# Latents' gates four blocks at a time in the banks of rows' sums, those banks then holding the input of the u products, and context's v rows on VectorE

## The chip, the cores and the metric

The kernel runs on one core of a Trainium2 chip. The metric is the device time of one execution in microseconds (us); of several runs the median is taken.

## The reference, cut to what matters

A two-layer backbone in float32 over 256 context tokens and 256 latent tokens, width 1024. In the kernel these are four tiles of 128 tokens: tiles 0 and 1 are context, 2 and 3 latents. In each layer four branches (two attentions, a convolution, a pooling) are merged under gates, and then a layer of experts follows, in which each token takes 128 rows of 1024 numbers out of a table u and 128 out of a table v (8 heads, 16 rows each, out of 16384 rows):

```python
def merge_branches(h, ys, w_gate, b_gate, w_branch, w_out):
    acc = jax.nn.sigmoid(h @ w_gate[0] + b_gate[0]) * (ys[0] @ w_branch[0])
    for n in range(1, N_BRANCH):
        acc = acc + jax.nn.sigmoid(h @ w_gate[n] + b_gate[n]) * (ys[n] @ w_branch[n])
    return acc @ w_out

def peer_ffn(h, wq, k1, k2, u_tab, v_tab):      # for 128 tokens xc
    ...
    u = jnp.take(u_tab, idx, axis=0)
    act = jax.nn.gelu(jnp.einsum('td,thkd->thk', xc, u), approximate=False)
    v = jnp.take(v_tab, idx, axis=0)
    return jnp.einsum('thk,thkd->td', gate * act, v)
```

Context goes through the experts in the first layer only, so there are six gathers of 128 slots (one slot: one u row and one v row for each of 128 tokens): here called C0, L0, L1, C1 (first layer: context tile 0, latent tiles 2 and 3, context tile 1) and F0, F1 (second layer, latents).

## The kernel before, in words

**Order.** The program is written out in one function, and the order of its lines is the order in which work is offered to the engines. It starts with context's first layer (`both` on `hc`). Then latents' first layer runs, with gather C0 laid between its products: `pump(us)` counts up the products' time and at every SLOT_US (2.9) steps the generator `gather` one slot on; `tick` does the same for pieces of attention, convolution and pooling in `pending`. Gathers L0 and L1 run alone, beside the router's selection of rows. C1 is laid between the products of latents' second layer, F0 begins beside the last products of that layer, and F1 runs alone to the end.

**A gather's slot.** `u_slot` (L1128) has GpSimd issue an indirect DMA (L1124) of one u row per token into a place of tag "u", and VectorE multiply it with the tile's normed input `self.h2` and sum it up (L1132). `v_slot` (L1142) fetches the v rows 16 slots later. A v row is either added up on VectorE into `dacc` (L1149), or ScalarE makes a diagonal matrix of its weights (L1154) and TensorE adds two products of 512 columns up in PSUM (L1156). `on_dve` says which: P_C0 sends 122 of C0's rows to VectorE, `few` a quarter, `half` a half, `most` (C1) three quarters; the last row is always TensorE's. At the end `add` (L1166) weighs the sums and adds them to X, once for `dacc` and once for PSUM. `prepare` (L1102) makes `h2` out of X, in SBUF, with a product and a sum (L1110, L1113).

**PSUM.** All eight banks have a tag: mm (2 tiles of one bank), at (2), tr (2) and va (one tile of two banks, the v rows' sums, held through a whole gather).

**Gates.** In latents' first layer `both` (L954) loads, for each half c of the columns and branch n, one weight tile of w_branch and two of w_gate (1024 x 256 each), all 1 MB in the three places of tag "w". It goes block by block: `gate_mm` (8 products of 256 columns, then a tanh on ScalarE), then `branch_mm` (4 products, then VectorE's product with the gate, L941, and sum, L942). In the second layer `both_quads` (L967) does four blocks at a time: `gate_quad` loads two tiles of w_gate (512 x 512 each) and runs half of the depth of all four blocks out of the first and the other half out of the second, into two mm tiles, followed by four tanh; then w_branch is loaded, and two times two blocks of branch products go into a tr tile (L975), each followed by one product and one sum on VectorE with 512 columns (L984, L985). The gates of four blocks stand in two tiles of tag t2, of which there are four, and from which attention takes its own tiles too.

## Time and profile before

| | us |
|---|---|
| median of 3 runs | 3176.56 |
| lowest, highest | 3165.32, 3186.99 |
| the profiled execution | 3168.74 |
| its span | 3167.0 |

The profile is of one execution. Busy time over the span: TensorE 75%, VectorE 74%, GpSimd 56%, ScalarE 21%; the kernel moves 1036 MB, 327 GB/s on the mean. These are averages over stages with different limits, so the profile is read by stage. The stages stand in it at: latents' first layer with C0 about 415 to 1020 us, L0 to 1410, L1 to 1800, latents' second layer with C1 to 2280, the end of that layer to 2380, F0 to 2790, F1 to the end. "POOL" in a row is GpSimd, "PE" TensorE, "DVE" VectorE, "ACT" ScalarE, "SP" the queue that loads weights.

### The profile page before, as it was taken

The numbers are of one execution on the slowest core, as the hardware profiler recorded it, in microseconds if no ns is written. First come the engines' busy times: TensorE is split into PE (matmuls) and PEld (weight loads), VectorE is DVE, ScalarE is ACT, GpSimd is POOL, SyncE is SP. The second block draws the span as 40 slices with busy tenths as digits, with TensorE's granted clock in tenths as the row PEclk, the third lists the DMA queues.
The fourth block names the chain that finished last, engine by engine and source line by source line (L and its number), as shares of the span: only waits on it lengthen the run. The fifth ranks groups of instructions, "written<-read, shape, count | busy, mean of one in ns | idle before, by whom it ended". The sixth has DMA issues, their size and how long they took to land.

```text
span 3167.0 us, 32196 instructions
## 1 busy us (share of the span) xinstructions
PE 2376.9 (75%) x10264; PEld 1586.2 (50%) x10264; DVE 2357.8 (74%) x5204; ACT 654.6 (21%) x1543; POOL 1789.3 (56%) x1542
## 2 busy tenths in 40 slices
PE   7999989898877785665455589899997966645555
PEld 5879878666666452222111267667696522211111
DVE  5977679678968899747666769977567985566666
ACT  3454321233112211110000211123332211100001
POOL 0000057443556687776777757766205777777775
PEclk9999999899988897886777789899998988876767
DMA  9948979787999899998999999999838989999998
GB/s 305 334 161 285 304 263 351 270 296 250 339 331 356 321 392 364 336 381 294 373 369 369 338 343 389 341 388 386 300 107 288 323 324 372 372 344 372 383 377 300
DMA packets 397863, 1036.48 MB, mean 327 GB/s; under 512 B 30464, under 2 KB 169216, under 8 KB 397696
## 3 DMA queue, kind: packets, MB, share of 16 engines
q0 software_dynamic: 221184, 805.40, 68.0%
q1 hardware_dynamic: 173072, 226.25, 21.0%
q10 hardware_dynamic: 3440, 2.78, 0.3%
q8 instruction: 82, 1.34, 0.2%
q14 instruction: 85, 0.70, 0.1%
HBM read 1032.22 MB, written 2.10 MB: 327 GB/s over the span
## 4 chain that ended last, share of the span: by engine, by line
PE 33%; DVE 18%; issue 17%; DMA 15%; POOL 15%; ACT 1%; another core or an unknown queue 0%; POOLq 0%; SPq 0%; ACTq 0%; DVEq 0%
PE mm L218 11%; POOL u L1124 8%; POOL v L1124 7%; DMA v<-in_v_dram,idx 7%; DVE u L1132 5%; PE va L1156 4%; DMA w<-in_w_gate_dram 3%; PE mm L214 3%; PE mm L216 2%; PE mm L215 2%; PE mm L916 2%; DMA u<-in_u_dram,idx 2%; DVE dacc L1149 2%; PE at L531 2%; DVE m L832 2%
## 5 line engine op out<-in xcount | busy, mean ns | idle before, releaser
L1124 POOL DMA_INDIRECT u<-in_u_dram,idx x768 | 869.7, 1132 | 926.4 <-DVE m L862 409.0
L1156 PE MATMUL va<-v,dg 128*128 128x512 f32 x1436 | 890.5, 763 | 554.5 <-DMA v<-in_v_dram,idx 379.8
L1132 DVE SCALAR_TENSOR_TENSOR u<-u,h 128x1024 f32<-128x1024 f32 x768 | 933.2, 1219 | 338.1 <-DMA u<-in_u_dram,idx 307.6
L1124 POOL DMA_INDIRECT v<-in_v_dram,idx x768 | 919.1, 1197 | 433.6 <-issue 193.9
L1156 PEld LDWEIGHTS va<-v,dg 128*128 128x128 f32 x1436 | 315.8, 237 | 1070.4 <-issue 925.6
L1149 DVE SCALAR_TENSOR_TENSOR dacc<-v,wt,dacc 128x1024 f32<-128x1024 f32 x403 | 515.6, 1279 | 105.9 <-DMA v<-in_v_dram,idx 78.6
L218 PE MATMUL mm<-hT,w 128*128 128x256 f32 (+1 forms) x1664 | 383.4, 385 | 71.4 <-DMA w<-in_w_gate_dram 50.9
L218 PEld LDWEIGHTS mm<-hT,w 128*128 128x128 f32 x1664 | 312.4, 207 | 130.2 <-issue 53.6
L1154 ACT ACTIVATE dg<-ident,wt 128x128 f32<-128x128 f32 x359 | 141.3, 400 | 1029.9 <-PE va L1156 524.7
L832 DVE SCALAR_TENSOR_TENSOR m<-m,cols,m 128x256 f32<-128x256 f32 x360 | 158.2, 473 | 0.1
L916 PE MATMUL mm<-hT,w 128*128 128x256 f32 x512 | 134.5, 405 | 14.5 <-DVE t L453 6.6
L215 PE MATMUL mm<-hT,whi 128*128 128x256 f32 x512 | 143.4, 280 | 0.0
L214 PE MATMUL mm<-hT,whi 128*128 128x256 f32 x448 | 128.0, 286 | 3.1 <-ACT whi L176 3.1
L216 PE MATMUL mm<-hT,whi 128*128 128x256 f32 x448 | 127.2, 284 | 1.8 <-DVE whi L177 1.8
L218 PE MATMUL mm<-w,hT 128*128 128x256 f32 x512 | 117.1, 388 | 10.6 <-DMA w<-in_w_in_dram 10.6
L916 PEld LDWEIGHTS mm<-hT,w 128*128 128x128 f32 x512 | 97.6, 202 | 34.5 <-issue 17.2
L177 DVE TENSOR_TENSOR whi<-w,whi 128x1024 fp32r<-128x1024 f32 x86 | 103.6, 1220 | 13.8 <-ACT whi L176 6.5
L218 PEld LDWEIGHTS mm<-w,hT 128*128 128x128 f32 x512 | 99.1, 195 | 26.4 <-issue 12.5
L176 ACT CAST whi<-w 128x1024 fp32r<-128x1024 f32 x86 | 87.4, 1047 | 51.3 <-PE mm L216 20.6
L215 PEld LDWEIGHTS mm<-hT,whi 128*128 128x128 f32 x512 | 97.0, 190 | 0.4 <-issue 0.3
L214 PEld LDWEIGHTS mm<-hT,whi 128*128 128x128 f32 x448 | 85.3, 190 | 8.8 <-ACT whi L176 4.2
L216 PEld LDWEIGHTS mm<-hT,whi 128*128 128x128 f32 x448 | 84.8, 189 | 7.2 <-DVE whi L177 3.7
(361 smaller groups left out, 2960.9 us busy)
## 6 DMA issues: line engine op xcount, KB each, us to landing
w<-in_w_gate_dram SPq DMA_DIRECT2D x48, 1024.0 KB
w<-in_w_in_dram SPq DMA_DIRECT2D x42, 1024.0 KB
X<-in_w_mod_dram SPq DMA_DIRECT2D x40, 512.0 KB
wm<-in_w_mod_dram SPq DMA_DIRECT2D x40, 512.0 KB
w<-in_w_branch_dram SPq DMA_DIRECT2D x20, 1024.0 KB
w<-in_w_q_dram SPq DMA_DIRECT2D x20, 1024.0 KB
u<-in_u_dram,idx POOLq DMA_INDIRECT x768
v<-in_v_dram,idx POOLq DMA_INDIRECT x768
```

The source lines that it names most:

```text
L177: nc.vector.tensor_tensor(lo.bitcast(FR), v, hi, op=OP.subtract)
L214: nc.tensor.matmul(ps, ah, bh, start=first, stop=False)
L215: nc.tensor.matmul(ps, ah, bl, start=False, stop=False)
L216: nc.tensor.matmul(ps, al, bh, start=False, stop=last)
L218: nc.tensor.matmul(ps, a[:, kb, ca], b[:, kb, cb], start=first, stop=last)
L832: nc.vector.scalar_tensor_tensor(acc[:, b, :], yb[:, b, k:k + T], cols[:, l, cw + k:cw + k + 1], acc[:, b, :], op0=OP.mult, op1=OP.add)
L916: nc.tensor.matmul(ps, a[:, kb, ca], b[:, k0 + kb, cb], start=f, stop=z, skip_group_check=True)
L1124: nc.gpsimd.indirect_dma_start(out=r, out_offset=None, in_=table, in_offset=bass.IndirectOffsetOnAxis(ap=self.idx[:, j:j + 1], axis=0))
L1132: nc.vector.scalar_tensor_tensor(r, r, 1.0, self.h2, op0=OP.mult, op1=OP.mult, accum_out=self.act[:, j % 16:j % 16 + 1])
L1149: nc.vector.scalar_tensor_tensor(self.dacc, v, w, self.dacc, op0=OP.mult, op1=OP.add)
L1154: nc.scalar.activation(dg, ident, AF.Copy, scale=w)
L1156: nc.tensor.matmul(self.va[:, half, :], dg, v[:, half * 512:(half + 1) * 512], start=j == self.pe[0], stop=j == self.pe[-1])
```

## The change

Four things, the third of which follows from the second:

- Latents' first layer calls `both_quads` in place of `both`, with the ticks and pumps per block as they were.
- `gate_quad` puts its four blocks into the two banks of va, and `both_quads` its branch products into mm tiles in place of tr tiles (both layers).
- These banks are then free for the gathers of latents: the last sum of `prepare` writes `h2` of a latent tile into va, where L1132 reads it for 128 rows; the sums of v rows on TensorE go into two at tiles. For context `h2` stays in SBUF.
- Context's gathers C0 and C1 have no row on TensorE: all 128 v rows are summed up on VectorE, and there is one `add` in place of two. That takes 6 rows of C0 and 33 of C1 (every fourth and the last) off TensorE.

```diff
@@ -919,7 +919,9 @@ gate_quad
-        ps = [mm_ps() for i in range(2)]
+
+        ps = va_ps()
+        ps = [ps[:, :512], ps[:, 512:]]
@@ -972,7 +974,7 @@ both_quads
-                    pb = tr_ps()
+                    pb = mm_ps()
@@ -1101,22 +1103,25 @@ Tile
         def prepare(self, found=False):
 
-            self.h2 = sb.tile([128, D], F, tag="h2", name="h2", bufs=2)
+            h2 = sb.tile([128, D], F, tag="h2", name="h2", bufs=2)
+
+            self.h2 = va_ps() if self.t > 1 else h2
...
-                nc.vector.scalar_tensor_tensor(self.h2[:, c], X[:, self.t, c], rst2[:, self.t:self.t + 1], ps,
+                nc.vector.scalar_tensor_tensor(h2[:, c], X[:, self.t, c], rst2[:, self.t:self.t + 1], ps,
                                                op0=OP.mult, op1=OP.mult)
                 ps = bcast(tr_ps(), modc[self.l][:, self.s, 24 + half * 4:28 + half * 4])
-                nc.vector.tensor_tensor(self.h2[:, c], self.h2[:, c], ps, op=OP.add)
+                nc.vector.tensor_tensor(self.h2[:, c], h2[:, c], ps, op=OP.add)
 
         def begin(self, on_dve):
 
-            self.pe = [j for j in range(128) if not on_dve(j) or j >= 128 - LAST]
+
+            self.pe = [j for j in range(128) if not on_dve(j) or j >= 128 - LAST] if self.t > 1 else []
             self.dv = [j for j in range(128) if j not in self.pe]
-            self.va = va_ps().rearrange("p (a b) -> p a b", a=2)
+            self.va = [at_ps() for half in range(2)] if self.pe else None
...
                 if j == self.dv[-1]:
-                    self.add(self.dacc)
+                    self.add([self.dacc[:, :512], self.dacc[:, 512:]])
...
-                    nc.tensor.matmul(self.va[:, half, :], dg, v[:, half * 512:(half + 1) * 512],
+                    nc.tensor.matmul(self.va[half], dg, v[:, half * 512:(half + 1) * 512],
...
-        t.add(t.va.rearrange("p a b -> p (a b)"))
+        if t.pe:
+            t.add(t.va)
...
-    P_C0, P_L0, P_L1, P_C1, P_F0, P_F1 = (lambda j: j < 48 or (j * 15) % 16 < 15), few, half, most, few, half
+    P_L0, P_L1, P_F0, P_F1 = few, half, few, half
...
-    behind.append(gather(tsc[0], P_C0, None, rc))
+    behind.append(gather(tsc[0], None, None, rc))
@@ -1426,17 +1432,17 @@ latents, first layer
-    both(h, ys, T, 0, (3,), accT, True)
+    both_quads(h, ys, 0, (3,), accT, True)
...
-    both(h, ys, T, 0, (0,), accT, False)
+    both_quads(h, ys, 0, (0,), accT, False)
...
-    both(h, ys, T, 0, (1,), accT, False)
+    both_quads(h, ys, 0, (1,), accT, False)
...
-    both(h, ys, T, 0, (2,), accT, False)
+    both_quads(h, ys, 0, (2,), accT, False)
...
-    behind.append(gather(tsc[1], P_C1))
+    behind.append(gather(tsc[1], None))
```

## Rows read from the trace of the kernel before

**Rows 1.** Busy time by stage (columns: stretch, length, each engine's busy us, clock, DMA share, GB/s)

```profile
620.00:925.00 305.00, 259.34 (x1188) 206.76 (x1188) 250.85 (x579) 76.11 (x180) 143.54 (x122) 0.92 0.82 293
1020.00:1300.00 280.00, 196.21 (x567) 108.70 (x566) 268.10 (x892) 50.19 (x118) 208.81 (x170) 0.84 0.95 356
1300.00:1410.00 110.00, 75.12 (x147) 29.61 (x146) 58.91 (x87) 14.27 (x38) 86.52 (x78) 0.86 0.97 358
1410.00:1800.00 390.00, 208.24 (x314) 73.84 (x312) 256.57 (x377) 35.67 (x93) 287.26 (x262) 0.71 0.94 353
1990.00:2280.00 290.00, 265.85 (x1183) 196.45 (x1182) 214.80 (x366) 81.23 (x205) 181.01 (x147) 0.94 0.95 357
2600.00:2790.00 190.00, 128.95 (x243) 50.66 (x244) 96.82 (x142) 24.87 (x62) 139.00 (x133) 0.84 0.97 367
...
1500.00:1550.00 50.00, 25.67 (x36) 8.58 (x36) 35.33 (x51) 3.03 (x8) 38.11 (x40) 0.78 1.03 407
```

**Rows 2.** TensorE's waits, 600 to 930 us (total us, times, longest)

```profile
PE mm L218 <- DMA w<-in_w_gate_dram: 44.8, 8, 13.6
```

**Rows 3.** Timeline, 884 to 908 us, TensorE and then SP (start, length)

```profile
885.41 1.89 PE L218 MATMUL mm<-ys,w 128*128 128x256 f32 x8
900.91 6.52 PE L218 MATMUL mm<-hT,w 128*128 128x256 f32 x16 [13.61 <-DMA w<-in_w_gate_dram]
...
885.61 2.09 SPq L231 DMA_DIRECT2D w<-in_w_gate_dram  x2
```

**Rows 4.** Groups by line, 605 to 925 us (count | busy, mean ns | idle before)

```profile
L694 DVE TENSOR_REDUCE st<-at 128x1 f32<-128x512 f32 x16 | 11.0, 686 | 12.5 <-PE at L531 12.2 <-issue 0.3
L697 ACT ACTIVATE t<-at,st 128x512 f32<-128x512 f32 x16 | 11.0, 691 | 6.2 <-DVE st L695 6.2
L941 DVE SCALAR_TENSOR_TENSOR th<-th,mm 128x256 f32<-128x256 f32 x24 | 9.9, 411 | 19.4 <-PE mm L218 19.3
```

**Rows 5.** The chain that ended last, 1450 to 1750 us, shares by line

```profile
by line: issue 41.7%; POOL u L1124 23.2%; POOL v L1124 21.7%; DMA v<-in_v_dram,idx 13.1%; PE va L1156 0.7%; POOLq L1124 0.0%
```

**Rows 6.** GpSimd's groups, 1450 to 1750, then 2820 to 3100; then its minimum/median/maximum

```profile
L1124 POOL DMA_INDIRECT v<-in_v_dram,idx x106 | 124.1, 1170 | 37.4 <-issue 30.5 <-remote 5.4 <-PE va L1156 0.9
L1124 POOL DMA_INDIRECT u<-in_u_dram,idx x106 | 107.8, 1017 | 32.3 <-issue 31.1 <-DMA v<-in_v_dram,idx 1.2
...
L1124 POOL DMA_INDIRECT v<-in_v_dram,idx x100 | 109.0, 1090 | 41.0 <-issue 27.4 <-remote 11.7 <-PE va L1156 0.9
L1124 POOL DMA_INDIRECT u<-in_u_dram,idx x100 | 101.3, 1013 | 30.5 <-issue 30.2 <-DMA v<-in_v_dram,idx 0.3
...
L1124 POOL DMA_INDIRECT u<-in_u_dram,idx x106: 933/938/1797, 1451.0 to 1749.7; - x106
```

**Rows 7.** Timeline of VectorE and GpSimd at the end of C0

```profile
1014.55 0.69 DVE L1170 TENSOR_TENSOR dacc<-dacc,g 128x512 f32<-128x512 f32 x1 [2.08 <-issue]
...
1014.82 1.24 POOL L1124 DMA_INDIRECT u<-in_u_dram,idx  x1 [0.30 <-issue]
...
1019.35 0.68 DVE L1170 TENSOR_TENSOR dacc<-va,g 128x512 f32<-128x512 f32 x1
...
1019.35 0.94 POOL L1124 DMA_INDIRECT u<-in_u_dram,idx  x1 [0.30 <-issue]
```

**Rows 8.** Costliest groups of the page, the rows' products

```profile
L1132 DVE SCALAR_TENSOR_TENSOR u<-u,h 128x1024 f32<-128x1024 f32 x768 | 933.2, 1219 | 338.1 <-DMA u<-in_u_dram,idx 307.6
...
L1149 DVE SCALAR_TENSOR_TENSOR dacc<-v,wt,dacc 128x1024 f32<-128x1024 f32 x403 | 515.6, 1279 | 105.9 <-DMA v<-in_v_dram,idx 78.6
```

**Rows 9.** Groups by line and shape: one operation, 512 columns, SBUF alone and with PSUM

```profile
L304 DVE SCALAR_TENSOR_TENSOR msum<-wm,silc,msum 128x512 f32<-128x512 f32 x28 | 20.8, 743 | 0.0
...
L984 DVE SCALAR_TENSOR_TENSOR t<-t,tr 128x512 f32<-128x512 f32 x4 | 2.7, 684 | 7.2 <-PE tr L218 7.2
```

**Rows 10.** TensorE's groups by line, 1990 to 2280 us

```profile
L916 PE MATMUL mm<-hT,w 128*128 128x256 f32 x512 | 134.5, 405 | 14.5 <-DVE t L453 6.6 <-DMA w<-in_w_gate_dram 6.6 <-ACT t L931 1.1
L1156 PE MATMUL va<-v,dg 128*128 128x512 f32 x88 | 46.4, 652 | 5.5 <-DMA v<-in_v_dram,idx 5.2 <-issue 0.3
```

More of the change, by code (lines that the diff above doesn't have):

```diff
@@ L1102, in prepare @@
         def prepare(self, found=False):
-            self.h2 = sb.tile([128, D], F, tag="h2", name="h2", bufs=2)
+            h2 = sb.tile([128, D], F, tag="h2", name="h2", bufs=2)
+            self.h2 = va_ps() if self.t > 1 else h2
             if found:
-                nc.vector.tensor_copy(self.h2[:, ::512], self.idx[:, :2])
+                nc.vector.tensor_copy(h2[:, ::512], self.idx[:, :2])
             for half in range(2):
@@ L1169, in add @@
                 c = slice(half * 512, (half + 1) * 512)
-                nc.vector.tensor_tensor(self.dacc[:, c], v[:, c], self.g2[:, c], op=OP.mult)
+                nc.vector.tensor_tensor(self.dacc[:, c], v[half], self.g2[:, c], op=OP.mult)
                 nc.vector.tensor_tensor(X[:, self.t, c], X[:, self.t, c], self.dacc[:, c], op=OP.add)
```

## The prediction

> **What bounds the kernel now.** The first view to read is the busy time by stage [rows 1], since no engine is the limit throughout. Three kinds of stage stand there. In latents' first layer (620 to 925 us) TensorE is busy 259 of 305 us, VectorE 251, and the DMA engines move 293 GB/s, less than the 357 they move in the like stage of the second layer. From 1020 to 1300, where L0 runs beside the router's selection, VectorE is busy 268 of 280 us: it is the bound. In the gathers that run alone (1410 to 1800, 2600 to the end, and the end of L0 from 1300) no compute engine is full and the DMA share is 0.94 to 0.97, which looks like transfers.
>
> The chain of waits says otherwise for those [rows 5]: from 1450 to 1750 it runs along GpSimd, 45% its own instructions and 42% "issue", and only 13% a transfer. GpSimd's groups agree [rows 6]: nearly all idle time before its instructions is "issue", 0.3 us a piece, so it waits for no place and no index. It sets the pace, and one thing stretches it: an issue takes 0.94 us at the median for u rows, but up to 1.80, and 1.02 (u) and 1.17 (v) on the mean.
>
> What stretches it shows in the timeline [rows 7]. At 1014.82 an issue begins while VectorE runs L1170 with both inputs in SBUF: it takes 1.24 us and ends 0.82 us after VectorE's instruction. At 1019.35 another begins with the same L1170, one input now in PSUM: 0.94 us, undisturbed. So an issue that meets a VectorE instruction with two SBUF inputs is held until this ends, and one that meets an instruction with a PSUM input is not. L1132 (r and `h2`) and L1149 (v and `dacc`) are of the first kind.
>
> In latents' first layer the view to read is TensorE's waits: 44.8 us in 8 waits for w_gate between 600 and 930 us [rows 2]. The timeline shows one [rows 3]: the quad's last branch product begins at 885.41, SP issues the two next w_gate tiles only from 885.61 on, and TensorE stands 13.61 us. `both` uses its second w_gate tile and its w_branch tile up to the end of the four blocks, so two of the three places come free only then. The sixteen instructions behind the wait take 6.52 us, where eight of their size had taken 1.89: another 2.7 us.
>
> **The u products' input in PSUM.** This takes L1132 out of the first kind for 512 of 768 rows. By [rows 6] an undisturbed issue is 0.938 us; in L1 a slot loses 0.08 (u) and 0.23 (v), together 0.31 us, in F1 0.08 + 0.15 = 0.23. What part of it is L1132's I take by its share of VectorE's time in two-SBUF instructions [rows 8]: 1.22 us per slot against half a row's 1.28 where half the v rows are VectorE's (66%), against a quarter (79%) in L0 and F0. So L1 gives 128 x 0.31 x 0.66 = 26 us, F1 128 x 0.23 x 0.66 = 19. The ends of L0 and F0 have 78 and 133 issues [rows 1], 105 slots; at 0.27 x 0.79 they give 22. Sum 67 us, the upper end. The lower: the dacc products that stay may meet more issues than now. Issues start every 1.24 us, so each of 64 products a tile (1.28 us) can hold one, by half its length, 0.64 us at most: 41 us a tile, against 128 x 0.27 x 0.34 = 12 now. Twice 29 more would leave 9 us. I take 48, nearer the upper end, since VectorE's instructions there begin when rows land, at a distance from the issues that I have no reason to see grow worse. Can transfers follow? A row is 128 x 4 KB = 0.524 MB; at the 407 GB/s moved from 1500 to 1550 [rows 1] a slot takes 2.58 us, and the L1 stage now takes 390/131 = 2.98. So 0.2 to 0.3 us fit. Where VectorE is the bound (1020 to 1300) the same relief is worth nothing.
>
> The product itself: no row shows L1132's form with a PSUM input. The nearest, one operation at 512 columns, takes 743 ns out of SBUF alone and 684 with one input in PSUM [rows 9]. So it costs between 0 and 60 ns less, some 8 us where VectorE is the bound; I take 0, since a sum is written out here as well.
>
> A rule speaks against the move: the Trainium skill, "VectorE: DVE Perf Modes", section "The TRN2 errata", gives an instruction a fixed part of 58 cycles out of SBUF and 120 out of PSUM at 0.96 GHz, an estimate of 65 ns more for each of 512 products, 33 us of VectorE. By [rows 9] the sign is the other way, and the row decides.
>
> Making `h2` costs nothing more: the second sum of `prepare` writes PSUM in place of SBUF, on the engine that reads it, behind the tile before's last product. The v sums take two at tiles, whose other users (attention) are done by then.
>
> **Gates four at a time in the first layer.** In `both_quads` w_gate's first tile is done after a third of the quad and its second after two thirds, so each place comes free one after the other, some 15 us of TensorE's warm time ahead of its next use (two thirds of 22 us: 64 instructions of the gates and 32 of the branch, 1.89 us per eight). The second layer, which has this order, shows what is left: 6.6 us of waits for w_gate over 8 quads [rows 10]. So 38 us of waits can go, and with them most of 8 x 2.7 us of slow blocks: 60 us of TensorE, the upper end. But VectorE, at 251 of 305 us, has only 54 us to give, and 5 of C0's v rows come to it (6 us) while 48 products and sums of 256 columns become 24 of 512 (about as much back). Its idle time that hangs on TensorE is 19.4 us before L941 and 12.2 before L694 [rows 4], the attention's maxima: 32 us. If DMA reached the second layer's 357 GB/s the stage would shrink by 305 x (1 - 293/357) = 55. Lower end 0, upper 55; I take 30, the idle time that TensorE causes.
>
> Other edits of this part go together: ticks and pumps per quad are equal; branch products in mm tiles give tr to attention; the quads' next start waits for the fourth tanh behind the va tile, hidden by the branch products but in the four quads of `gates`, some 0.5 us each.
>
> **Context's v on VectorE.** C1 gives VectorE 33 x 1.28 = 42 us, and takes 132 matmuls from TensorE. From 1990 to 2280 VectorE is busy 215 of 290 us and TensorE 266 [rows 1], of which these rows are 46 [rows 10]. The fuller engine is relieved, the emptier loaded. Between 20 us less (DMA at 383 in place of 357 GB/s) and 42 more (all of it exposed): I take 0, and 5 less for the end, where the last row's wait for TensorE and the second `add` (4 x 0.68 us) go.
>
> **Sum.** 48 + 30 + 5 = 83 us off the profiled execution's 3168.74: 3086. That execution is 7.8 us under the median, so 3092 against 3176.56.
>
> **The rivals.**
>
> *The transfers are the bound after all.* For it: a DMA share of 0.94 to 0.97 in the gathers. Against it: the 50 us at 407 GB/s and 1.25 us per issue, and the chain. Then 48 falls away: 3141. The Trainium skill, "DMA: Bandwidth & Descriptors", section "Specifications", states about 358 GB/s of HBM for a core, by which this would hold; the rows at 367 and 407 GB/s disagree.
>
> *VectorE fills up in the first layer.* For it: 251 of 305 us, and its products wait in order behind rows. Then the 30 us fall away: 3122.
>
> *Attention starves for t2 (slower).* A quad's gates hold two of four t2 tiles, and a unit of attention needs two. If the 24 units of the four quads at 620 to 790 us (16 of the window, 8 of the other) could no longer overlap, each would show its hand-overs: four steps of 0.69 us [rows 4], two of them behind a row product of 1.25, 5.3 us. All 24 cost 127 us: 3220. It takes 16 of 24 to eat up the gain, 22 to be slower by over 1%. Against it: the second layer's quads run beside attention with the same four tiles, and TensorE waits little there [rows 10].
>
> **How the numbers follow.** Forecast 0.60 (its own range 3060 to 3115), transfers bound 0.14, VectorE full 0.15, starved 0.07, and 0.04 that both gains fail (3170). 1%, about what a measurement of this kernel can tell from no change, is 32 us: 3145. Faster takes the forecast, 3122, and half of 3141: 0.79 with what lies at the edges; same 0.14; slower 0.07. The terms at their upper ends, 67 + 55 + 25, give 3030, at their lower ends 3210; 8 in 10 lie between 3040 and 3150, which holds the first two rivals.
>
> **What would show it.** Right: GpSimd's mean issue in the gathers of latents falls from 1.01 and 1.17 towards 0.95 and 1.05, L1's stage from 390 to some 360 us, GB/s there to 380 or more; TensorE's wait for w_gate in the first layer falls under 15 us. Wrong: issues stay as long (the lock isn't L1132's), or shorten while GpSimd begins to wait for places (transfers); TensorE's waits turn to VectorE or ScalarE in the first layer; C1's stage grows.

## The result, and the profile after

| | before | after |
|---|---|---|
| median, us | 3161.12 of 20 runs (3140.80 to 3186.99) | 3178.55 of 20 runs (3166.86 to 3195.19) |
| the profiled execution, us | 3168.74 | 3167.57 |
| ratio of after to before | | 1.0051, 95% interval 1.0033 to 1.0069 |

The prediction was 3092 us in a range of 3040 to 3150. The kernel got 17 us slower, outside the range and on the other side of no change. The two profiled executions are one run each, equal to 1.2 us, and the 20 runs of one kernel spread over 46 and 28 us: the two traces can't show the 17 us themselves, only in which stages time was won and lost.

Busy time of the changed kernel over the stretches of [rows 1] (stretch, length, each engine's busy us, clock, DMA share, GB/s):

```profile
620.00:925.00 305.00, 264.61 (x1186) 215.01 (x1185) 250.59 (x554) 73.17 (x172) 146.22 (x125) 0.88 0.83 304
1020.00:1300.00 280.00, 189.11 (x545) 105.32 (x546) 265.22 (x886) 48.02 (x117) 161.56 (x165) 0.84 0.93 348
1300.00:1410.00 110.00, 80.51 (x174) 33.32 (x172) 64.69 (x99) 15.74 (x40) 79.33 (x79) 0.84 0.98 371
1410.00:1800.00 390.00, 201.60 (x329) 73.34 (x330) 263.84 (x406) 39.63 (x102) 282.68 (x268) 0.72 0.95 360
1990.00:2280.00 290.00, 233.77 (x1130) 186.50 (x1129) 236.61 (x387) 78.92 (x204) 170.69 (x144) 0.88 0.97 361
2600.00:2790.00 190.00, 130.41 (x254) 52.24 (x255) 99.97 (x147) 25.94 (x64) 132.20 (x133) 0.82 0.97 369
```

GpSimd is busy 162 us in place of 209 from 1020 to 1300, so its issues did get shorter. But little followed: GB/s in the stretch of L1 is 360 (353 before), in that of F0's end 369 (367). Its groups in L1 and in F1, over the windows of [rows 6], and then its waits in F1 show where the gain went (groups: count | busy, mean ns | idle before; waits: total us, times, longest):

```profile
L1129 POOL DMA_INDIRECT u<-in_u_dram,idx x104 | 114.3, 1099 | 31.7 <-issue 28.9 <-DMA v<-in_v_dram,idx 2.4 <-DVE u L1137 0.3
L1129 POOL DMA_INDIRECT v<-in_v_dram,idx x107 | 108.4, 1013 | 46.3 <-issue 31.0 <-remote 13.7 <-DVE u L1137 0.9
```

```profile
L1129 POOL DMA_INDIRECT u<-in_u_dram,idx x99 | 104.3, 1053 | 30.2 <-issue 29.2 <-DMA v<-in_v_dram,idx 0.9
L1129 POOL DMA_INDIRECT v<-in_v_dram,idx x99 | 96.9, 978 | 49.7 <-issue 32.6 <-remote 16.8 <-PE at L1161 0.3
```

```profile
POOL v L1129 <- remote: 16.8, 8, 4.6
POOL u L1129 <- DMA v<-in_v_dram,idx: 0.9, 3, 0.3
```

Against [rows 6] a v issue in L1 fell from 1.170 to 1.013 us, a u issue rose from 1.017 to 1.099, since more of them now meet a sum into `dacc` (issues lose 27 us to these in L1, 13 before, worked out of the two traces). Per slot the two issues and GpSimd's idle time are 1.099 + 1.013 + 31.7/104 + 46.3/107 = 2.85 us, where before they were 1.017 + 1.170 + 32.3/106 + 37.4/106 = 2.84. What left the issues came back as idle time: "remote" is a wait whose releaser the trace doesn't name, 4.6 us at the longest in F1. (A semaphore is the counter by which one engine tells another that its work is done; it rises by an update.) The semaphore that rose last in each of these waits of over 0.3 us is TensorE's, which gives back the place of a v row, and it rose more than 1.5 us after the last TensorE instruction that raises it had ended. It was no row that landed late: from the end of an issue to the end of its row's last DMA packet it takes 4.75 us at the median in L1 here, and 4.70 in e6 below, the fastest run (slots 32 to 112).

TensorE's waits in latents' first layer, to be held against [rows 2]:

```profile
PE mm L218 <- DMA w<-in_w_branch_dram: 12.6, 5, 5.5
PE mm L218 <- DMA w<-in_w_q_dram: 10.3, 3, 3.7
PE va L916 <- DMA w<-in_w_gate_dram: 4.0, 1, 4.0
PE tr L553 <- DVE t L712: 4.0, 2, 3.4
PE tr L563 <- DVE ys L731: 3.5, 2, 3.1
```

The waits for w_gate fell from 44.8 to 4.0 us as reckoned, but w_branch, which is now asked for last, and w_q after it are waited for 22.9, and attention's hand-overs (L553, L563) appear.

The rows' products on the page of the changed kernel, to be held against [rows 8]:

```profile
L1137 DVE SCALAR_TENSOR_TENSOR u<-u,va 128x1024 f32<-128x1024 f32 x512 | 618.2, 1215 | 244.0 <-DMA u<-in_u_dram,idx 203.4
...
L1154 DVE SCALAR_TENSOR_TENSOR dacc<-v,wt,dacc 128x1024 f32<-128x1024 f32 x442 | 566.4, 1281 | 84.5 <-DMA v<-in_v_dram,idx 67.9
...
L1137 DVE SCALAR_TENSOR_TENSOR u<-u,h 128x1024 f32<-128x1024 f32 x256 | 311.5, 1218 | 16.3 <-DMA u<-in_u_dram,idx 15.8
```

By stage (worked out of both traces from the start of each gather's first u product; the last one to the end), in us:

```
            C0    L0     L1     C1     F0     F1
before    587.1 406.8  379.5  587.5  409.7  377.0
after     578.2 421.6  356.2  589.4  425.5  373.2
change     -8.9 +14.8  -23.3   +1.9  +15.8   -3.8
```

So there is a gain in C0 (the gates) and in L1 and F1 (the PSUM input), and a loss of the same size in L0 and F0, the two gathers beside the router. The experiments ask what each part is worth, and why the one gain is small and the loss there at all.

### The profile page after: what moved, and what is told of

It is laid out like the page before. It is cut to its first block, busy times and chain, and to the rows that moved or that the text cites. A ratio compares the mean times of both kernels' runs of the same rounds, so it can differ in the third digit from the quotient of the medians.

```text
span 3165.8 us, 31874 instructions
## 1 busy us (share of the span) xinstructions
PE 2327.0 (74%) x10108; PEld 1577.8 (50%) x10108; DVE 2390.4 (76%) x5207; ACT 640.1 (20%) x1504; POOL 1651.0 (52%) x1542
## 4 chain that ended last, share of the span: by engine, by line
PE 35%; DVE 21%; issue 16%; POOL 12%; DMA 11%; ACT 2%; another core or an unknown queue 2%; SPq 0%; ACTq 0%; POOLq 0%; DVEq 0%
PE mm L218 10%; DVE u L1137 7%; POOL u L1129 6%; POOL v L1129 5%; PE va L916 5%; PE at L1161 5%; DVE dacc L1154 3%; PE mm L214 3%; DMA w<-in_w_branch_dram 3%; PE mm L216 2%; PE mm L215 2%; DMA v<-in_v_dram,idx 2%; PE at L531 2%; DMA u<-in_u_dram,idx 2%
## 5 line engine op out<-in xcount | busy, mean ns | idle before, releaser
L1161 PE MATMUL at<-v,dg 128*128 128x512 f32 x1280 | 795.9, 769 | 519.2 <-DMA v<-in_v_dram,idx 231.4
L1129 POOL DMA_INDIRECT v<-in_v_dram,idx x768 | 816.1, 1063 | 483.6 <-issue 188.0
L1137 DVE SCALAR_TENSOR_TENSOR u<-u,va 128x1024 f32<-128x1024 f32 x512 | 618.2, 1215 | 244.0 <-DMA u<-in_u_dram,idx 203.4
L1161 PEld LDWEIGHTS at<-v,dg 128*128 128x128 f32 x1280 | 286.0, 239 | 997.0 <-issue 850.3
L1137 DVE SCALAR_TENSOR_TENSOR u<-u,h 128x1024 f32<-128x1024 f32 x256 | 311.5, 1218 | 16.3 <-DMA u<-in_u_dram,idx 15.8
L218 PE MATMUL mm<-hT,w 128*128 128x256 f32 (+1 forms) x1152 | 254.7, 377 | 42.8 <-DMA w<-in_w_q_dram 12.6
L916 PE MATMUL va<-hT,w 128*128 128x256 f32 x1024 | 260.8, 403 | 23.3 <-DMA w<-in_w_gate_dram 16.3
L218 PEld LDWEIGHTS mm<-hT,w 128*128 128x128 f32 x1152 | 212.0, 209 | 85.7 <-issue 28.1
L916 PEld LDWEIGHTS va<-hT,w 128*128 128x128 f32 x1024 | 198.9, 202 | 59.2 <-DMA w<-in_w_gate_dram 18.1
L218 PEld LDWEIGHTS mm<-w,hT 128*128 128x128 f32 x512 | 99.8, 197 | 24.5 <-issue 10.1
L215 PEld LDWEIGHTS mm<-hT,whi 128*128 128x128 f32 x512 | 97.5, 190 | 0.4 <-issue 0.3
```

Source lines behind the costliest of these rows:

```text
L215: nc.tensor.matmul(ps, ah, bl, start=False, stop=False)
L218: nc.tensor.matmul(ps, a[:, kb, ca], b[:, kb, cb], start=first, stop=last)
L916: nc.tensor.matmul(ps, a[:, kb, ca], b[:, k0 + kb, cb], start=f, stop=z, skip_group_check=True)
L1129: nc.gpsimd.indirect_dma_start(out=r, out_offset=None, in_=table, in_offset=bass.IndirectOffsetOnAxis(ap=self.idx[:, j:j + 1], axis=0))
L1137: nc.vector.scalar_tensor_tensor(r, r, 1.0, self.h2, op0=OP.mult, op1=OP.mult, accum_out=self.act[:, j % 16:j % 16 + 1])
L1161: nc.tensor.matmul(self.va[half], dg, v[:, half * 512:(half + 1) * 512], start=j == self.pe[0], stop=j == self.pe[-1])
```

## The experiments

All ratios are to the kernel before on the same chip. The runs fell on five chips, and this turned out to matter as much as the largest part of the change: the kernel before took 3104, 3100 and 3103 us on those of e1 to e4, e5 to e8 and e17 to e18 (chips 7, 2 and 5), and 3171 and 3185 on those of e9 to e12 and e13 to e16 (chips 4 and 10); the first measurement, 3161, is like the latter.

### One part alone, one part undone

e1 puts the first layer's gates alone into the kernel before, e2 the v rows of context; e3 and e4 undo one part of the changed kernel. (The calls for the other three branches change alike.)

```diff
e1 (kernel before)
-    both(h, ys, T, 0, (3,), accT, True)
+    both_quads(h, ys, 0, (3,), accT, True)
...
e2 (kernel before)
-            self.pe = [j for j in range(128) if not on_dve(j) or j >= 128 - LAST]
+            self.pe = [j for j in range(128) if not on_dve(j) or j >= 128 - LAST] if self.t > 1 else []
...
e3 (changed kernel)
-            self.h2 = va_ps() if self.t > 1 else h2
+            self.h2 = h2
e4 (changed kernel)
-    both_quads(h, ys, 0, (3,), accT, True)
+    both(h, ys, T, 0, (3,), accT, True)
...
```

> The kernel before with one part of the change: latents' first layer calls both_quads in place of both (gates in mm tiles, branch products in tr tiles, as the second layer had it). The prediction's theory: TensorE's waits for w_gate go, 30 us faster, ratio 0.990. Theory A (the waits only change their name: w_branch is now asked for last and comes late): 0 to 15 us faster, ratio 0.995 to 1.000, with waits for w_branch in place of w_gate. Theory B (attention starves for t2 tiles): 10 us slower or more, ratio over 1.003, with attention's hand-overs at the end of the chain of waits from 620 to 790 us.

> The kernel before with one part of the change: context's gathers C0 and C1 have no v row on TensorE. The prediction's theory: no cost in the stage and 5 us less at its end, ratio 0.998. Theory C (this part is what makes the changed kernel slower): its 39 products of 1.28 us on VectorE, 50 us of work, lie partly on the path; 10 to 25 us slower, ratio 1.003 to 1.008, and C1's stage grows.

> The changed kernel with one part undone: h2 of a latent tile is written to SBUF and read there, so all u products have two SBUF inputs again. The prediction's theory: 48 us slower than the changed kernel, ratio 1.020 against the kernel before. Theory D (transfers set the pace of the gathers, and GpSimd's shorter issues only make it wait): within 8 us of the changed kernel, ratio 1.003 to 1.008, with issues as long as in the kernel before and fewer waits of GpSimd for landed rows. Theory E (the PSUM input itself is what costs): faster than the changed kernel by 10 us or more, ratio 1.002 or less.

> The changed kernel with one part undone: latents' first layer calls both again, block by block; the u products' input stays in PSUM and context's v on VectorE. The prediction's theory: 30 us slower than the changed kernel, ratio 1.015. Theory A: 0 to 15 us slower than the changed kernel, ratio 1.005 to 1.010. Theory B: faster than the changed kernel by 10 us or more, ratio 1.002 or less.

| | median, us | ratio, 95% interval |
|---|---|---|
| e1, quads alone | 3132.36 | 1.0095 (1.006 to 1.0131) |
| e2, context's v alone | 3119.32 | 1.0038 (1.0001 to 1.0075) |
| e3, all but the PSUM input | 3090.45 | 0.995 (0.9916 to 0.9983) |
| e4, all but the first layer's quads | 3066.29 | 0.9896 (0.986 to 0.9932) |

The parts don't add up: two that cost 29 and 15 us alone give together, with the banks of va for the gates, 13 us less (e3; the same kernel again gives 1 less in e7 and 5 less in e17). The quads alone are slower although w_gate's wait has gone down to 2.9 us. TensorE's longest waits in e1, 600 to 930 us:

```profile
PE mm L218 <- DMA w<-in_w_q_dram: 26.4, 3, 10.3
PE at L531 <- ACT t L697: 4.1, 1, 4.1
PE tr L563 <- DVE ys L731: 4.0, 1, 4.0
```

C0 lasts 606.6 us there against 587.1 in the first trace of the kernel before (588.2 in e5's). The quad's gates then hold both mm tiles and its branch products share tr with attention; where gates go to va and branch products to mm, and all else of the first layer is as changed, it lasts 574.7 (e3), 588.8 (e7) and 582.9 (e17), three traces of one kernel. That these banks make the difference follows from the comparison; which of the two does was not tried. The ratio is the one of theory B, but attention's hand-overs are 4 us a line and w_q's 26.4 us are longer than any of them, so its reason, the t2 tiles, is not shown. For e2 the loss is in C0 (601.2) and C1 (600.0 us; 587.5 and 579.4 in two traces of the kernel before). Theory C stands, with the addition that with the gates' new banks C1 takes 583 to 588 us (e3, e6, e7, e17).

By what was expected e3 and e4 would speak for theories E and B, as long as the changed kernel is taken to be at 1.005. On this chip it isn't, as the next four show.

### The changed kernel itself on such a chip

> The kernel before, unchanged, looked at once beside the next three. Packets of row transfers that took over 0.2 us in place of 0.159 to 0.169 were frequent in some stretches of every earlier trace (some 365 GB/s) and nearly absent in others (410 GB/s, 2.56 us per slot). Theory D1 (the kernel's own order of issues makes them): they stand in the same slots as in the first trace of this kernel, in L1 from 1540 to 1800 us and in most of F1. Theory D2 (they come from outside the kernel's program): they stand elsewhere, and slots with and without them change places.

> The changed kernel, unchanged, on the chip of the runs beside it. Prediction's theory: 0.973 of the kernel before. Theory D (gathers go at the transfers' pace): where the long packets are rare the GpSimd relief is seen, F1 344 us in place of 371 as between e4_blocks and e3_h2sbuf, and the ratio is 0.985 or less; where they are frequent the ratio is 1.00 to 1.01 as first measured.

> e3_h2sbuf again: the changed kernel with the u products' input in SBUF, now beside the changed kernel itself. The difference of the two is the worth of the PSUM input. Prediction's theory: 48 us slower than e6_after. Theory D: 10 to 40 us slower where long packets are rare, within 8 us where they are frequent. Theory E: faster than e6_after.

> e4_blocks again: the changed kernel with latents' first layer block by block, beside the changed kernel. By the slots' times of the earlier traces C0 ends 14 us later than with the quads (1014.3 against 999.9 and 996.2 us), so theory A and the prediction's theory expect it 10 to 30 us slower than e6_after; theory B expects it faster.

Kernels e5 and e6 are the kernel before and the changed kernel, e7 and e8 those of e3 and e4.

| | median, us | ratio, 95% interval |
|---|---|---|
| e6, the changed kernel | 3043.85 | 0.9835 (0.9799 to 0.9872) |
| e7, h2 in SBUF | 3099.21 | 0.9987 (0.9954 to 1.002) |
| e8, first layer by blocks | 3065.62 | 0.9893 (0.9854 to 0.9931) |

On this chip the change is worth 56 us. The PSUM input is worth 55 (e7 less e6, medians; by stage the two traces differ by 57 in L0, L1, F0 and F1, and by 15 in C0, which that input doesn't touch), the quads 22 (e8 less e6). For the PSUM input that is nearer to the prediction's 48 than to theory D's 10 to 40. GpSimd's groups in L1, the kernel before and then the changed one (e6's window reaches into L1's last 16 slots, which have v rows only):

```profile
L1124 POOL DMA_INDIRECT v<-in_v_dram,idx x88 | 104.3, 1186 | 26.8 <-issue 25.0 <-PE va L1156 1.8
L1124 POOL DMA_INDIRECT u<-in_u_dram,idx x87 | 94.2, 1083 | 26.5 <-issue 25.9 <-DMA v<-in_v_dram,idx 0.6
```

```profile
L1129 POOL DMA_INDIRECT v<-in_v_dram,idx x105 | 108.0, 1029 | 32.0 <-issue 30.8 <-PE at L1161 1.2
L1129 POOL DMA_INDIRECT u<-in_u_dram,idx x90 | 84.3, 937 | 27.5 <-issue 27.5
```

This is what the prediction said should be seen: u issues from 1.083 to 0.937, v from 1.186 to 1.029, idle time nothing but "issue". Per slot that is 2.88 us before and 2.58 after, and the window's GB/s went from 364 to 407. The changed kernel over this window and one in F1, in the columns of [rows 1]:

```profile
1450.00:1700.00 250.00, 144.59 (x207) 45.59 (x208) 174.12 (x240) 21.77 (x57) 190.82 (x195) 0.77 1.03 407
2820.00:3000.00 180.00, 96.98 (x142) 32.37 (x143) 129.29 (x189) 16.78 (x43) 137.92 (x139) 0.83 1.02 407
```

By stage, L1 took 331.2 us in place of 371.6, F1 344.8 in place of 360.7, and L0 384.8 in place of 399.0.

Theories D1 and D2 ask where the long packets come from: from 2800 to 2900 us the kernel before moved 360 GB/s in its first trace and 410 in e5, and in e12 and e16 376 and 355. The stretches of long packets come and go with the execution, so D1 falls; that they come from outside the program (D2) isn't shown by this.

### Half the bytes

Rows of L1 and F1 with half the numbers, in both kernels, beside the two unchanged; the products read the half twice. These four ran on a chip of the other kind (e10 twice only).

```diff
e9 (changed kernel), e10 (kernel before)
+            if self.t == 3:
+                half_of = table.rearrange("n (a d) -> (n a) d", a=2)
+                nc.gpsimd.indirect_dma_start(out=r[:, 512:], out_offset=None, in_=half_of,
+                                             in_offset=bass.IndirectOffsetOnAxis(ap=self.idx[:, j:j + 1], axis=0))
+                return r
...
+            if self.t == 3:
+                b = r[:, None, 512:].to_broadcast([128, 2, 512])
...
```

> The changed kernel with rows of half the width in L1 and F1: each u and v row brings 512 numbers in place of 1024 (2 KB a token), and the products read them twice, so that every instruction on the engines keeps its length; the sums of these two tiles are others than the reference's. Transfers have then half the bytes and can't be the limit there; what is left is GpSimd's pace. Prediction's theory: issues every 1.25 us, 2.50 to 2.55 us per slot in the middle of L1 and F1, with some of it by the sums into dacc that stay. Theory D says the same of this kernel, and that the changed kernel itself stands at 2.56 only where long packets are rare.

> The kernel before with the same half rows in L1 and F1 (the sums of these two tiles are others than the reference's). If VectorE's products with two SBUF inputs hold GpSimd's issues by 0.2 to 0.3 us a slot by themselves, as the prediction reckoned, these slots take 2.65 to 2.8 us with no transfer limit, 0.15 to 0.25 more than in e9_after_half, 20 to 30 us in each tile. Rival F: the hold costs little by itself (2.50 to 2.60 us, under 0.1 more than e9_after_half), and the kernel before is slow in its gathers through long packets, which late issues bring about or prolong.

> The changed kernel again, to see how the ratio goes with the chip. Theory D: the ratio goes with the long packets, 0.98 to 0.985 where its gathers run at 2.56 us per slot, 1.00 to 1.01 where they run at 2.8 to 2.9. A ratio of 1.00 with slots at 2.56, or of 0.985 with slots at 2.9, would speak against it.

> The kernel before, unchanged, one look on the chip of the three beside it. Theory D2: its stretches of long packets lie elsewhere than in e5_before and in the first trace; theory D1: in the same slots.

| | median, us | ratio, 95% interval | us per slot, from u product 32 to 112 of L1, F1 |
|---|---|---|---|
| e9, changed, half rows | 3174.02 | 1.002 (0.9984 to 1.0055) | 2.79, 2.87 |
| e10, before, half rows | 3207.28 | 1.0117 (1.0069 to 1.0166) | 3.05, 3.07 |
| e11, changed | 3176.77 | 1.0016 (0.9993 to 1.004) | 2.82, 2.81 |
| e12, before | one run | | 2.84, 2.96 |

GpSimd's groups from 1450 to 1700 us, in L1, first e9 and then e10:

```profile
L1131 POOL DMA_INDIRECT u<-in_u_dram,idx x88 | 96.4, 1096 | 26.8 <-issue 17.7 <-DMA u<-in_u_dram,idx 3.7 <-DVE u L1146 3.0
L1131 POOL DMA_INDIRECT v<-in_v_dram,idx x87 | 89.7, 1031 | 37.1 <-issue 21.8 <-PE at L1177 8.1 <-DMA u<-in_u_dram,idx 2.4
```

```profile
L1126 POOL DMA_INDIRECT v<-in_v_dram,idx x82 | 101.0, 1231 | 25.0 <-issue 22.0 <-DMA u<-in_u_dram,idx 1.5 <-DMA v<-in_v_dram,idx 1.2
L1126 POOL DMA_INDIRECT u<-in_u_dram,idx x83 | 100.2, 1208 | 25.3 <-issue 21.0 <-DMA u<-in_u_dram,idx 2.1 <-DMA v<-in_v_dram,idx 1.8
```

With half the bytes (183 GB/s in e9 from 1450 to 1700) no slot got shorter by more than 0.03 us; those of the kernel before got longer. The bytes are not the limit on this chip. The level that I expected (2.5 us) was missed in both: in e10 more issues meet a VectorE product (1.21 and 1.23 us an issue), in e9 the sums into dacc hold them (1.10 and 1.03) and GpSimd waits 8.1 us for places that TensorE gives back. That rows which land sooner (2.3 us after the issue, against 4.6 to 4.8 in e11) put VectorE's products elsewhere between the issues is a guess. The difference has the size that the prediction reckons: 0.20 to 0.26 us a slot, 33 us between the two kernels (by stage 43 in L1 and 31 in F1, of which C1 and F0 take back 30 and 19). The hold is real and the PSUM input lifts it on this chip too; rival F falls.

e11 beside e12 repeats the first measurement's picture, and its ratio is the one that theory D gave for slots at 2.8 us; by e9 it is not the bytes that bring it. By stages the changed kernel is 7 us shorter in L1 and 18 in F1, and 18 longer in L0, 19 in C1 and 22 in F0; the two executions differ by 30 us where the medians differ by 6, so these are rough.

### No hold at all

All v rows of L1 and F1 summed up on TensorE, so that no product with two SBUF inputs is left there but, in e15, the u products.

```diff
e13 (changed kernel), e15 (e3's kernel)
-    P_L0, P_L1, P_F0, P_F1 = few, half, few, half
+    P_L0, P_L1, P_F0, P_F1 = few, share(0, 2), few, share(0, 2)
```

> The changed kernel with all v rows of L1 and F1 summed up on TensorE, so that no VectorE product with two SBUF inputs meets an issue in these two gathers. Theory G (the holds left by dacc set the pace): 2.5 to 2.6 us per slot in L1 and F1 on any chip; where the changed kernel runs at 2.8 to 2.9 that is 25 to 35 us a tile less, ratio 0.98 to that kernel. Theory H (rows land no faster there): the slots stay at 2.8 to 2.9 with issues of 0.94 us, and GpSimd's waits for landed rows grow; ratio 1.00 to the changed kernel. Where the changed kernel already runs at 2.56 both say no change.

> The changed kernel, on the same chip as e13_after_te: 0.98 to 0.985 of the kernel before where its L1 and F1 run at 2.56 us per slot, 1.00 to 1.01 where they run at 2.8 to 2.9.

> As e13_after_te, but with the u products' input in SBUF: of the two kinds of hold only theirs is left in L1 and F1. Theory G: 2.6 to 2.75 us per slot, 10 to 25 us a tile slower than e13_after_te. Theory H: like e13_after_te where rows land at 2.8 to 2.9 us per slot.

> The kernel before, one look on the chip of the three beside it, for its slots in L1 and F1: 2.8 to 2.9 us per slot.

| | median, us | ratio, 95% interval | us per slot, L1, F1 (as above) |
|---|---|---|---|
| e13, changed, v on TensorE | 3225.24 | 1.0121 (1.0074 to 1.0169) | 2.81, 2.83 |
| e14, changed | 3193.67 | 1.0038 (1.0011 to 1.0065) | 2.88, 2.82 |
| e15, h2 in SBUF, v on TensorE | 3197.96 | 1.0058 (1.0028 to 1.0088) | 3.02, 2.84 |
| e16, before | one run | | 2.85, 2.86 |

GpSimd's groups in e13 from 2820 to 3000 us, in F1:

```profile
L1129 POOL DMA_INDIRECT u<-in_u_dram,idx x68 | 65.1, 957 | 20.7 <-issue 19.2 <-DMA v<-in_v_dram,idx 0.6 <-DMA u<-in_u_dram,idx 0.6
L1129 POOL DMA_INDIRECT v<-in_v_dram,idx x58 | 54.9, 946 | 40.8 <-remote 17.3 <-issue 12.5 <-PE at L1161 10.1
```

Hardly an issue is held any more (0.957 and 0.946 us), and still a slot takes 2.83 us: GpSimd stands before its v issues instead, 17.3 us without a named releaser and 10.1 for places that TensorE gives back. G falls. The pace that H forecast came, its reason did not: rows land 4.9 us after their issue in these slots, in e6 4.7, and the waits without a name all end with TensorE's semaphore, as in the first measurement. What neither theory had: e13 is 32 us slower than e14, and 27 slower than e15 (9 to 35 by resampling the runs), where the u products still hold the issues. By stages e13 against e15 loses 20 us in L0 and 17 in F0 and wins 3 and 2 in L1 and F1. The two differ in the place of `h2` alone, so on this chip the PSUM input costs more beside the router than it gives in the gathers that run alone.

### What stands on the one kind of chip and not on the other

VectorE's waits from 1000 to 1110 us, the start of L0, in the changed kernel (e11) and in the kernel before (e12) on one chip:

```profile
DVE dacc L1175 <- ACT g L1169: 12.3, 1, 12.3
DVE dacc L1175 <- issue: 5.2, 1, 5.2
DVE pk L1059 <- remote: 4.6, 1, 4.6
DVE mx L1016 <- remote: 3.3, 2, 1.8
```

```profile
DVE mx L1011 <- issue: 6.0, 2, 4.9
DVE u L1132 <- DMA u<-in_u_dram,idx: 2.3, 4, 1.2
```

VectorE is the bound of this stage [rows 1], and it stands here behind ScalarE's L1169, which waits 21.1 us without a named releaser. L1169 copies two tiles that TensorE's L1181 makes, and TensorE's semaphore is all that it waits for. The second of the two products, and the two copies (e11; start, length, idle before):

```profile
998.29 1.16 PE L1181 MATMUL tr<-ident,modc 128*128 128x128 f32 x8
1005.21 0.59 ACT L1169 COPY g<-tr 128x512 f32<-128x512 f32 x1 [6.98 <-remote]
1019.93 0.59 ACT L1169 COPY g<-tr 128x512 f32<-128x512 f32 x1 [14.13 <-remote]
```

The product ends at 999.45; the second copy starts 20.5 us later. In between the trace has four TensorE instructions that raise its semaphore, which end at 998.00, 999.45, 1001.61 and 1013.49, and four rises, at 1005.19, 1019.90, 1020.01 and 1020.17: each copy starts 0.02 to 0.03 us after a rise. Elsewhere a rise comes 0.014 us after its instruction's end at the median. So the work was done and the word of it came late. TensorE in the same time:

```profile
1001.66 1.89 PE L218 MATMUL mm<-hT,w 128*128 128x256 f32 x8
1004.50 0.59 PE L218 MATMUL mm<-hT,w 128*128 128x256 f32 x2 [0.95 <-issue]
1005.91 0.38 PE L218 MATMUL mm<-hT,w 128*128 128x256 f32 x1 [0.82 <-issue]
1008.00 0.59 PE L218 MATMUL mm<-hT,w 128*128 128x256 f32 x1 [1.71 <-issue]
1010.10 0.58 PE L218 MATMUL mm<-hT,w 128*128 128x256 f32 x1 [1.51 <-issue]
1011.50 0.58 PE L218 MATMUL mm<-hT,w 128*128 128x256 f32 x1 [0.81 <-issue]
1012.90 0.58 PE L218 MATMUL mm<-hT,w 128*128 128x256 f32 x1 [0.82 <-issue]
```

These are the products of a block, which have nothing to wait for once the block is begun; eight had taken 1.89 us just before. From 1004.50 on they come 1.2 to 2.1 us apart. In these 11 us GpSimd issues one row after the other, all but one without a hold. Why the semaphore rises late the trace doesn't say. Over the whole kernel it sets the two kinds of chip apart. The table has, from 420 to 3000 us, the idle time put down to "issue" or "remote" (worked out of each engine's waits); how many of the 1,536 x 16 = 24,576 semaphore updates of landed rows the whole trace holds; and how many rises of TensorE's and of VectorE's semaphore came over 1 us after the last instruction of that engine that raises it:

```
                        TensorE  ScalarE  GpSimd remote  landings   late rises:
                                                         recorded   TensorE VectorE
before, first trace       122      466        8            16,713     31      0
after, first trace        200      744       47            13,119     83     20
e12 before (chip 4)       131      445       34            17,739     28      0
e11 after  (chip 4)       269      707       45            13,178     66     28
e10 before, half rows      50      263        9            20,124     18      0
e9 after, half rows (4)   182      643       27            13,734     87     13
e16 before (chip 10)      103      488       28            16,491     27      2
e14 after  (chip 10)      346      727       61            12,766     95     21
e15 h2 in SBUF (10)       149      500       27            15,827     47      0
e13 PSUM       (10)       233      665       79            13,525     99     16
e5 before  (chip 2)         0        0        0            24,574      0      0
e6 after   (chip 2)        11        0        0            24,576      0      0
```

On chips 2, 5 and 7 (e1 to e8, e17, e18) TensorE has 29 us of such idle time at most and ScalarE none, all landings but two are recorded, and no rise of this stretch is late. On the others a fifth to a half of the landings' records are missing, and some of the engines' own rises; rises come late, and with the PSUM input more of them do. They lie where the time was lost: in L0 4 to 9 of TensorE's rises are late with `h2` in SBUF and 16 to 40 with it in PSUM, in F0 3 to 11 and 18 to 24.

The first two columns are no measure of lost time: where the record of a rise is missing, an ordinary wait loses its name too. Of e11's 269 us of TensorE 183 stand before v products, of ScalarE's 707 some 460 before the diagonal matrices. Idle time before TensorE instructions that wait for nothing, as above, is 1.7 to 7.9 us in the five traces of those chips with the PSUM input and none in all others. The late rises are not the record's alone, since the engine that waits starts only behind them. The landings that lack a record did take place: every trace has all 24,576 packets of 4 bytes, sixteen to an issue, and in e6, where all landings are recorded, each follows such a packet by 0.3 to 0.9 us.

That denser issues of GpSimd bring the late rises is theory K below; VectorE's reading of PSUM beside TensorE's writing goes with the same edit, and no run separates the two.

> The changed kernel with the u products' input in SBUF (as e3_h2sbuf and e7_h2sbuf). Theory K (where engines stand without a shown cause, denser issues of GpSimd bring more of it, so the PSUM input costs what it saves): on such a chip this kernel is faster than the changed kernel, 0.99 to 1.00 of the kernel before against 1.002 to 1.005, with less of TensorE's and ScalarE's idle time put down to issue. The prediction's theory: slower than the changed kernel by 30 to 50 us on any chip. On a chip without such stands both expect 0.995 to 1.00 as in e3 and e7.

> The changed kernel with latents' first layer block by block (as e4_blocks and e8_blocks). If the quads are worth 20 us on any chip, as between e6 and e8: 1.008 to 1.012 of the kernel before on a chip with stands, 0.99 on one without. If they are worth nothing where engines stand: 1.002 to 1.005.

These two are e3's and e4's kernels on chip 5, which is of the kind without late rises: 1.0001 (0.9964 to 1.0039), median 3097.86, and 0.9898 (0.9862 to 0.9934), median 3069.84. They repeat e7 and e8 on a third chip and say nothing on theory K. What speaks for its result, not for its reason, is e13 against e15 and the late rises of the table.

## Why the prediction was wrong

**The u products' input, 48 us.** On a chip without late rises mechanism and size were right: 55 us (e7 less e6), with issues at the lengths forecast. On the chip of the measurement the step that failed is the sentence "Where VectorE is the bound (1020 to 1300) the same relief is worth nothing". It was not nothing: L0 and F0, for whose ends 22 us of gain stand in the upper bound of 67, became longer by 31 us together (40 in e11, 24 in e14). L1 and F1, for which the other 45 stand there, became shorter by 27, 25 and 15 us. With `h2` in PSUM the semaphores by which TensorE, and in part VectorE, release the others rise late more often, most clearly in these two stages; only the place of `h2` changed between e15 and e13, and it cost 27 us. Why they rise late is open.

Two smaller steps of this term failed with it. The sums into `dacc` were to meet no more issues than before, "at a distance from the issues that I have no reason to see grow worse"; they held L1's issues for 27 us in place of 13, and F1's for 20 in place of 14. And "Can transfers follow?" looked at bytes, from one stretch of 50 us at 407 GB/s [rows 1]. Rows landed as soon as on chip 2; what GpSimd came to wait for were places behind late rises, and with nearly all holds gone (e13) the slots stayed at 2.8 us. The sign stood in the trace of before: 95 us of ScalarE's waits there are "remote", a name that no wait has on chips 2, 5 and 7, while the prediction read the idle time of GpSimd alone [rows 6].

**The rivals.** *The transfers are the bound* came nearest: as its sign said, issues became shorter while GpSimd began to wait for places. Its mechanism, the bytes, is refuted by e9, and the places were TensorE's to give back. Among the cases there was none in which the relief costs something elsewhere, and the one for slower, attention starved for t2, is not what came: attention's waits in the changed kernel are 4.0 us and less a line.

**The product itself.** 1215 ns with PSUM, 1218 without: nothing, as taken. The 60 ns that [rows 9] seemed to show are not PSUM's: the 743 ns form takes a factor for each partition out of a tile, the 684 ns form does not. Two more groups of the kernel before have it the other way round, with a factor from a tile and a PSUM input, and with neither:

```profile
L1110 DVE SCALAR_TENSOR_TENSOR h<-X,few_cols,tr 128x512 f32<-128x512 f32 x12 | 8.9, 738 | 4.7 <-PE tr L1176 4.0 <-issue 0.6
L367 DVE SCALAR_TENSOR_TENSOR m<-X 128x512 f32<-128x512 f32 x12 | 8.2, 684 | 0.0
```

The estimate of 65 ns more for PSUM, from the Trainium skill's figures ("VectorE: DVE Perf Modes", section "The TRN2 errata"), doesn't show in this form either.

**The hold.** Issues take 1.2 us in e10 and 0.95 in e13, where no product in L1 and F1 has two SBUF inputs. The Trainium skill ("SBUF — State Buffer", section "Who interferes with whom") puts a DMA that seems to be held by a VectorE operation down to GpSimd, kept from generating descriptors; these lengths agree. Its remedy, another queue, was not tried here.

**Gates, 30 us.** w_gate's waits went (44.8 to 4.0 us), C0 became 9 us shorter in the first pair, 15 on chip 2, 1 and 3 on chips 4 and 10; against blocks the quads are worth 22 us (e8). The term was mis-sized, as half of the waits went over to w_branch and w_q. "Other edits of this part go together" failed: without va and mm for the quads they cost 29 us (e1), so the banks were no side matter. In the first measurement's traces 9 us of the 30 came.

**Context's v, 5 us less.** Wrong in sign: 15 us more alone (e2), inside the bounds of 20 less and 42 more that the prediction drew, and smaller in C1 with the gates' new banks (583 to 588 us against e2's 600).

**The sum.** On chip 2 the parts make 55 + 22 - 15 (e2, on another chip) = 62 us, against 56 measured and 83 predicted. That this comes near is in part luck, since the parts are not independent (e1, e2 and e3). On the chips with late rises the changed kernel is 6 to 17 us slower.

## What to carry to other kernels

Before a relief is priced, look in the trace of before at every engine's waits for such as have no named releaser ("remote", in a kernel that runs on one core), and for missing records: where they were here (8 us on GpSimd, 95 on ScalarE), the relief cost as much beside the router as it gave. Idle time put down to "issue" needs care: with records missing it holds ordinary waits. When an engine begins to wait for places, ask who gives them back before the transfers are blamed. A change of a few parts that share PSUM banks is to be measured with and without each on one chip; alone, two of these three parts were slower.

## What the hardware showed that was not expected

- Chips differ by 2% on the same program (3100 to 3104 us on three, 3161 to 3185 on three measurements), and in the sign of a change: 0.9835 on one, 1.0016 to 1.0051 on the others.
- On the chip without late rises where it was looked at the changed kernel moved 407 GB/s through most of L1 and F1 (e6). The Trainium skill ("DMA: Bandwidth & Descriptors", section "Specifications") gives some 358 GB/s of HBM for a core, as half of what two cores share; this kernel runs on one and moved more.
- On the others TensorE's semaphore rose up to 20 us after the instruction that raises it had ended (0.014 us at the median), and TensorE went through products of one block 1.2 to 2.1 us apart in place of 0.24. Whether this comes from the supply of instructions, from the recording of the trace, whose records are missing on just these chips, from what other cores did, or from something else of the chip is open: no run here takes the one away and leaves the other.
